# The opening loads of an encoder trunk: three parameter rows first, on ScalarE's queue, and the other rows later

## The chip, the cores and the metric

The kernel runs on one core of a Trainium2 chip. A core has five engines that run in parallel and each work through their own list of instructions in order: TensorE (PE, with its weight loads as PEld), VectorE (DVE), ScalarE (ACT), GpSimd (POOL) and SyncE (SP), which here does nothing but issue transfers. ScalarE can issue transfers too. Sixteen DMA engines move the data between HBM and the on-chip memory. An instruction waits on semaphores for what it needs, and what stands behind it on the same engine waits with it. The metric is the device time of one execution in microseconds; the median of the timed runs counts.

## What is computed

A trunk of two layers on a sequence of 1024 positions with 1024 features, in float32. Each layer norms its input, modulates it with a shift and a scale that come from a conditioning vector c, mixes over the positions (layer 0 with forgetting attention, layer 1 with gated linear attention), and then runs a gated feed-forward block in the same frame. Cut to what the change touches:

```python
c_act = jax.nn.silu(c)
for i in range(DEPTH):
    mod = c_act @ ada_w[i] + ada_b[i]
    sh1, sc1, g1, sh2, sc2, g2 = jnp.split(mod, N_MOD, axis=-1)
    h = modulate(rms_norm(x, norm1_g[i]), sh1, sc1)
    y = mixer(h)                      # layer 0: proj = h @ w_in, split into q, k, v, f_logit
    x = x + g1[:, None, :] * y
    h = modulate(rms_norm(x, norm2_g[i]), sh2, sc2)
    x = x + g2[:, None, :] * swiglu(h, ffn_w_in[i], ffn_w_out[i])
return rms_norm(x, final_g)
```

So the first product of layer 0 needs the norm of x, the vectors sh1 and sc1 (two of the six blocks of c_act @ ada_w[0], plus ada_b), norm1_g, and the weights w_in. The vectors norm2_g, gla_g_o, gla_b_a, final_g and fox_b_f are needed later.

## The kernel before

Nearly all products are split: an operand is held as a rounded high part and a low part, and a product is three matmuls (`mm3`, L260 to L263). The features are cut into 8 blocks of 128, called d, and the sequence into two halves of 512 positions, hf 0 and 1.

**Who sets the order.** The program is written as one list of instructions; a scheduler, which simulates the kernel, turns it into one list for each engine. It follows the order of the text, but lets an instruction go ahead of others that are not ready in its simulation. `tied(ins)` (L265) holds the instructions of a block behind a given instruction of the same engine. All transfers from SP go through one list; the program tracks a transfer's completion with a semaphore.

**The opening (L335 to L373).** ScalarE issues four copies of c into `craw` (L338), 32 partitions each, which become `cblk` after a Silu (L369). SP issues, in the text's order: x tile 0; the small rows of c, gla_g_o, gla_b_a and final_g into `rows2` (L342 to L345); x tile 1; the rows of ada_b, norm1_g and norm2_g into `rows` (L348 to L350); x tiles 2 and 3; the ada weights of feature 0 (`load_ada0`, L328: four transfers of 256 KB, two column blocks j times two halves kh of the inner dimension); fox_b_f into `bf` (L355), 16 pieces of 4 bytes; the weights of f, of the first q and of the first k (L216, L199), each followed in the text by its split into high and low parts; the ada weights of features 1 and 2. Then PE transposes `rows2` and `rows` into one PSUM tile `vps` (L364, L365), ScalarE makes `cact` = Silu(c) of it (L368), and DVE copies it to `vec` (L370), in which all these vectors stand as columns.

**Norm of the first half.** `ss_half(0)` (L501): ScalarE squares x tiles 0 to 3 and sums (L504), DVE and POOL make the root (L506, L507), and DVE, ScalarE and POOL scale the four tiles (L511, L513, L515).

**The loop over features (L936 to L951).** For each d, `ada0_mod(d)` (L520) makes the shift and the scale of feature d: for d = 0, 1, 2 one half of the inner dimension on PE (L527) and the other on DVE (L533, L535), for d = 3 to 7 all on DVE; then PE sums over the partitions (L537), DVE adds ada_b (L538) and makes the multiplier (`make_a`, L386). `h_block` (L541) has PE transpose the four x tiles' blocks (L544), ScalarE apply scale and shift (L546) and round (L548), and DVE or POOL make the low part (L549). `first_k` (L554) adds feature d to the products of f, q and k, `first_v` (L920) those of v, one feature later. `load_ada0(d + 3)` is issued in `pre(d)`; the ada tiles go round a ring of eleven slots, two for a feature, so that the second tile of feature 5 and all of features 6 and 7 wait until an earlier feature has been used. The two halves of the v weights (wv_0 and wv_4) come from `feed.next()` at d = 0 and d = 2. At d = 4, x tiles 4 to 7 are loaded and `ss_half(1)` follows. Behind the loop come the evacuations of the first half (`first_evac`, L881) and the same for the second half, whose features need no further modulation.

Of the kernel before, what the change touches and what calls it, by code (L numbers as in the profile page):

```python
# [16 lines left out]
P = 128  # L17
S = 1024
D = 1024
# [35 lines left out]
def trunk(ctx, tc, x, c, ada_w, ada_b, norm1_g, norm2_g, ffn_w_in, ffn_w_out,  # L55
# [139 lines left out]
    def load_w(src, name, ws=ws, lo_p=3):  # L195
# [4 lines left out]
        leave_ffn()  # L200
        w = Pair(ws([P, kk, m], FR, name + "h"), ws([P, kk, m], FR, name + "l"))
# [135 lines left out]
    for q in range(4):  # L337
        nc.scalar.dma_start(craw[32 * q:32 * q + 32], c[0].rearrange("(r s) -> r s", s=32))  # L338
    load_x(0)
    rows2 = mrows[1][0:32]  # L340
    nc.vector.memset(rows2, 0.0)
    nc.sync.dma_start(rows2[0:8, :], c.rearrange("o (j p) -> (o j) p", p=P))  # L342
    nc.sync.dma_start(rows2[8:16, :], gla_g_o.rearrange("o (j p) -> (o j) p", p=P))
    nc.sync.dma_start(rows2[16:20, :], gla_b_a.rearrange("o (j p) -> (o j) p", p=P))
    nc.sync.dma_start(rows2[20:28, :], final_g.rearrange("(j p) -> j p", p=P))  # L345
    load_x(1)
    rows = mrows[0]
    nc.sync.dma_start(rows[0:96, :], ada_b.rearrange("l (j p) -> (l j) p", p=P))  # L348
    nc.sync.dma_start(rows[96:112, :], norm1_g.rearrange("l (j p) -> (l j) p", p=P))
    nc.sync.dma_start(rows[112:128, :], norm2_g.rearrange("l (j p) -> (l j) p", p=P))  # L350
    load_x(2)
    load_x(3)
    load_ada0(0)
    bf = cst.tile([16, 1], F32, name="bf")
    nc.sync.dma_start(bf, fox_b_f.rearrange("o h -> h o"))  # L355
    W = fox_w_in[0]
    wf = load_w16(W[:, 3 * D:3 * D + 16], "fw", wst)
    wq0 = load_w(W[:, 0:P], "wq0", wst)
    wk0 = load_w(W[:, D:D + P], "wk0", wst)
# [3 lines left out]
    vps = mp0([P, 160], F32, "vps")  # L363
    nc.tensor.transpose(vps[:, P:P + 32], rows2, ident[0:32, 0:32])  # L364
# [3 lines left out]
    nc.scalar.activation(cact, vps[:, P:P + 8], AF.Silu)  # L368
    nc.scalar.activation(cblk, craw, AF.Silu)  # L369
    nc.vector.tensor_copy(vec, vps)  # L370
    gocol = lambda k: vec[:, P + 8 + k: P + 9 + k]
    fgcol = lambda k: vec[:, P + 20 + k: P + 21 + k]
    bacol = lambda k: vec[:, P + 16 + k: P + 17 + k]  # L373
# [146 lines left out]
    def ada0_mod(d):  # L520

        npe = NPE[d]
        mp = mp0([P, 2], F32, f"mp{d}")
        part = lambda k: araw[(d, k // 4)][:, k % 4]
        for j in range(2):
            for k in range(npe):
                nc.tensor.matmul(mp[:, j:j + 1], part(k)[:, j, :], cact[:, k:k + 1], start=k == 0 and j == 0,  # L527
                                 stop=k == 7 and j == 1)
# [9 lines left out]
        nc.vector.tensor_add(modc[:, 0, 0:2, d], mp, vec[:, d:d + 16:8])  # L538
# [377 lines left out]
    ss_half(0)  # L916
    acc = first_acc(0)
# [1271 lines left out]
```

## Time and profile before

| | us |
|---|---|
| three timed runs: lowest, median, highest | 2394.7, 2395.99, 2396.03 |
| the profiled execution, as timed | 2396.32 |
| its span in the trace | 2394.6 |
| PE busy in the span | 2352.3 |
| moved by the DMA engines in the first 60 us | 16.46 MB |
| mean rate of the DMA engines in the first 60 us | 274 GB/s |
| mean rate over the span | 151 GB/s |

The granted clock of TensorE was 0.997 in the mean. In the timeline a row reads: start, duration, engine, line of the kernel, operation, out<-in, count; in brackets the engine's idle time ahead of it and what ended it. `SPq` and `ACTq` are the transfers as SP and ScalarE issue them: the duration is that of the issue, not of the transfer. In the list of waits a row reads: who waited <- for whom: us in total, times, longest. In the list of transfers it reads: out<-in, issuing engine, operation, count, size of each, median us from issue to landing.

### The profile page before, as it was taken

The numbers are of one execution on the slowest core, as the hardware profiler recorded it, in microseconds if no ns is written. First come the engines' busy times: TensorE is split into PE (matmuls) and PEld (weight loads), VectorE is DVE, ScalarE is ACT, GpSimd is POOL, SyncE is SP. The second block draws the span as 40 slices with busy tenths as digits, with TensorE's granted clock in tenths as the row PEclk, the third lists the DMA queues.
The fourth block names the chain that finished last, engine by engine and source line by source line (L and its number), as shares of the span: only waits on it lengthen the run. The fifth ranks groups of instructions, "written<-read, shape, count | busy, mean of one in ns | idle before, by whom it ended". The sixth has DMA issues, their size and how long they took to land.

```text
span 2394.6 us, 35920 instructions
## 1 busy us (share of the span) xinstructions
PE 2352.3 (98%) x12246; PEld 1999.3 (83%) x12246; DVE 1679.0 (70%) x2804; ACT 1184.6 (49%) x2285; POOL 1201.8 (50%) x1073
## 2 busy tenths in 40 slices
PE   7999999999999999999999999999999999999998
PEld 6888888878888888888888898898888888888888
DVE  6577777676697778775788655345596676775787
ACT  4665556666554444445324766564443433345326
POOL 3343344432437878763363466563345666653262
PEclk9999999999999999999999999999999999999999
DMA  9233333123335555447665244454434534357664
GB/s 275 72 107 115 94 110 115 59 93 106 128 108 191 168 167 172 154 171 267 226 226 178 76 142 120 118 155 153 130 100 154 172 128 144 137 182 260 228 201 146
DMA packets 329408, 361.89 MB, mean 151 GB/s; under 512 B 24508, under 2 KB 253016, under 8 KB 329224
## 3 DMA queue, kind: packets, MB, share of 16 engines
q1 hardware_dynamic: 329032, 359.57, 46.6%
q8 instruction: 97, 1.59, 0.3%
q14 instruction: 87, 0.71, 0.1%
q10 hardware_dynamic: 192, 0.02, 0.0%
HBM read 269.25 MB, written 90.24 MB: 150 GB/s over the span
## 4 chain that ended last, share of the span: by engine, by line
PE 83%; DVE 5%; DMA 4%; ACT 3%; issue 2%; POOL 1%; SPq 1%; DVEq 0%; POOLq 0%; ACTq 0%
PE p_b L263 15%; PE p_b L262 15%; PE p_b L261 15%; PE o_b L1058 2%; PE t_b L1044 2%; PE qk_b L261 2%; PE qk_b L263 2%; PE qk_b L262 2%; PE s_b L1013 1%; PE s_b L1014 1%; PE gr_b L262 1%; PE gr_b L261 1%; PE gr_b L263 1%; PE vps_b L261 1%; PE vps_b L262 1%
## 5 line engine op out<-in xcount | busy, mean ns | idle before, releaser
L165 DVE TENSOR_TENSOR o_s<-xv_s,o_s 128x512 fp32r<-128x512 f32 (+1 forms) x376 | 343.7, 917 | 83.1 <-ACT o_s L164 82.4
L164 ACT CAST o_s<-xv_s 128x512 fp32r<-128x512 f32 (+1 forms) x376 | 217.7, 586 | 308.1 <-PE p_b L263 239.9
L1024 POOL TENSOR_SCALAR lp_s<-lp_s,st 128x128 f32<-128x128 f32 (+7 forms) x128 | 97.6, 767 | 265.9 <-DVE st L1023 229.2
L262 PE MATMUL p_b<-B,o_s 128*128 128x512 f32 x576 | 224.3, 389 | 0.0
L263 PE MATMUL p_b<-B,o_s 128*128 128x512 f32 x576 | 223.9, 389 | 0.0
L261 PE MATMUL p_b<-B,o_s 128*128 128x512 f32 x576 | 223.2, 389 | 0.0
L785 POOL TENSOR_TENSOR ex_s<-xv_s,xv_s 128x512 f32<-128x512 f32 (+1 forms) x64 | 88.3, 1380 | 259.8 <-DMA xv_s<-in_ffn_w_in_dram 89.0
L261 PE MATMUL p_b<-T,o_s 128*128 128x512 f32 x480 | 186.8, 389 | 0.0
L262 PE MATMUL p_b<-T,o_s 128*128 128x512 f32 x480 | 186.8, 389 | 0.0
L263 PE MATMUL p_b<-T,o_s 128*128 128x512 f32 x480 | 180.8, 389 | 0.0
L1022 ACT ACTIVATE lp_s<-lp_s,st 128x128 f32<-128x128 f32 (+7 forms) x128 | 99.3, 777 | 61.2 <-DVE st L1018 58.9
L261 PEld LDWEIGHTS p_b<-B,o_s 128*128 128x128 f32 x576 | 108.1, 188 | 22.5
L263 PEld LDWEIGHTS p_b<-B,o_s 128*128 128x128 f32 x576 | 108.1, 188 | 22.4
L262 PEld LDWEIGHTS p_b<-B,o_s 128*128 128x128 f32 x576 | 108.1, 188 | 22.4
L164 ACT CAST pt_s<-t_b 128x512 fp32r<-128x512 f32 (+1 forms) x160 | 79.6, 547 | 75.2 <-PE t_b L1044 74.5
L787 POOL TENSOR_TENSOR xv_s<-ex_s,xv_s 128x512 f32<-128x512 f32 (+1 forms) x64 | 84.7, 1323 | 58.1 <-DVE o_s L165 55.0
L1410 DVE TENSOR_TENSOR ex_s<-ex_s,p_b 128x512 f32<-128x512 f32 x140 | 93.6, 680 | 25.9 <-PE p_b L263 25.4
L425 POOL TENSOR_TENSOR ad_s<-ad_s,ad_s 128x512 f32<-128x512 f32 x62 | 89.1, 1438 | 34.8 <-ACT ad_s L423 22.1
L165 DVE TENSOR_TENSOR pt_s<-t_b,pt_s 128x512 fp32r<-128x512 f32 (+1 forms) x160 | 96.9, 631 | 13.8 <-ACT pt_s L164 13.5
L261 PEld LDWEIGHTS p_b<-T,o_s 128*128 128x128 f32 x480 | 90.1, 188 | 18.7
L262 PEld LDWEIGHTS p_b<-T,o_s 128*128 128x128 f32 x480 | 90.1, 188 | 18.7
L263 PEld LDWEIGHTS p_b<-T,o_s 128*128 128x128 f32 x480 | 90.1, 188 | 18.7
(1998 smaller groups left out, 7488.6 us busy)
## 6 DMA issues: line engine op xcount, KB each, us to landing
xv_s<-in_ffn_w_in_dram SPq DMA_DIRECT2D x176, 256.0 KB, 3.2
hid_B<-x SPq DMA_DIRECT2D x70, 512.0 KB, 2.7
ad_s<-in_ada_w_dram SPq DMA_DIRECT2D x384, 64.0 KB, 2.0
hid_T<-x SPq DMA_DIRECT2D x36, 512.0 KB, 2.8
xv_s<-in_ffn_w_out_dram SPq DMA_DIRECT2D x96, 192.0 KB, 4.5
ada_s<-in_ada_w_dram SPq DMA_DIRECT2D x128, 128.0 KB, 2.7
xv_s<-in_ffn_w_out_dram SPq DMA_DIRECT2D x40, 256.0 KB, 2.8
T2o<-hid_T SPq DMA_DIRECT2D x18, 512.0 KB, 8.6
```

The source lines that it names most:

```text
L164: nc.scalar.copy(hi, src)
L165: nc.vector.tensor_sub(lo, src, hi.bitcast(F32))
L261: nc.tensor.matmul(ps, ah, bh, start=start, stop=False)
L262: nc.tensor.matmul(ps, ah, bl, start=False, stop=False)
L263: nc.tensor.matmul(ps, al, bh, start=False, stop=stop)
L425: nc.gpsimd.tensor_add(acc, acc, raw)
L785: nc.gpsimd.tensor_add(s1, a21, a22)
L787: nc.gpsimd.tensor_sub(a11, s1, a11)
L1022: nc.scalar.activation(lp, lp, AF.Exp, bias=mcur, scale=-1.0, accum_out=st[:, qi, 2:3])
L1024: nc.gpsimd.tensor_scalar(lp, lp, st[:, qi, 3:4], 1.0, op0=ALU.mult, op1=ALU.mult)
L1044: nc.tensor.transpose(tp[:, i, :], lps[qi][:, psl(2 * b + jj)], ident)
L1410: nc.vector.tensor_add(d, d if src is None else dest(G, src), ps)
```

## The change

ScalarE now issues three transfers at the start, into one tile `rows` of 120 rows: c, ada_b and norm1_g. SP's list begins with x tiles 0 and 1, the four ada transfers of feature 0, x tiles 2 and 3. The weights of f, q and k are loaded as before, but their splits (`split_w16`, `split_w`) stand behind `ss_half(0)` in the text, and ScalarE's part of them is tied behind its last instruction there. Only `rows` is transposed at the start, into `vec[:, 0:112]` and `cact`. The rows of norm2_g, gla_g_o, gla_b_a and final_g, `bf`, and the four transfers of `craw` go out on SP (`later_rows`) at the end of the turn d = 1; their transpose, the copy into `vec[:, 112:148]` and the Silu of `craw` (`later_vec`) stand behind the loop over features. PE's products for the modulation of feature 1 are tied behind the instruction of PE ahead of them in the text, the last transpose of feature 0; DVE's sum for feature 0 behind its scaling of the x tiles.

```diff
+    def split_w(raw, kk, m, name, ws, lo_p=3):
         w = Pair(ws([P, kk, m], FR, name + "h"), ws([P, kk, m], FR, name + "l"))
...
-    def load_w16(src, name, ws=ws):
-
-        raw = wr([P, 8, 16], F32, name)
-        nc.sync.dma_start(raw, src.rearrange("(k p) m -> p k m", p=P))
+    def split_w16(raw, name, ws=ws):
...
-    for q in range(4):
-        nc.scalar.dma_start(craw[32 * q:32 * q + 32], c[0].rearrange("(r s) -> r s", s=32))
+    rows, rows2 = mrows[0][0:120], mrows[1][0:36]
+    bf = cst.tile([16, 1], F32, name="bf")
+    nc.scalar.dma_start(rows[112:120, :], c.rearrange("o (j p) -> (o j) p", p=P))
+    nc.scalar.dma_start(rows[0:96, :], ada_b.rearrange("l (j p) -> (l j) p", p=P))
+    nc.scalar.dma_start(rows[96:112, :], norm1_g.rearrange("l (j p) -> (l j) p", p=P))
     load_x(0)
...
     load_x(1)
...
+    load_ada0(0)
     load_x(2)
     load_x(3)
-    load_ada0(0)
...
+    def later_rows():
+        nc.sync.dma_start(rows2[0:16, :], norm2_g.rearrange("l (j p) -> (l j) p", p=P))
+        nc.sync.dma_start(rows2[16:24, :], gla_g_o.rearrange("o (j p) -> (o j) p", p=P))
+        nc.sync.dma_start(rows2[24:28, :], gla_b_a.rearrange("o (j p) -> (o j) p", p=P))
+        nc.sync.dma_start(rows2[28:36, :], final_g.rearrange("(j p) -> j p", p=P))
+        nc.sync.dma_start(bf, fox_b_f.rearrange("o h -> h o"))
+        for q in range(4):
+            nc.sync.dma_start(craw[32 * q:32 * q + 32], c[0].rearrange("(r s) -> r s", s=32))
+
+    def later_vec():
+        vps = mp0([P, 36], F32, "vps2")
+        nc.tensor.transpose(vps, rows2, ident[0:36, 0:36])
+        nc.vector.tensor_copy(vec[:, 112:148], vps)
+        nc.scalar.activation(cblk, craw, AF.Silu)
...
-    vps = mp0([P, 160], F32, "vps")
-    nc.tensor.transpose(vps[:, P:P + 32], rows2, ident[0:32, 0:32])
-    nc.tensor.transpose(vps[:, 0:P], rows, ident)
-    vec = cst.tile([P, 160], F32, name="vec")
+    vps = mp0([P, 120], F32, "vps")
+    nc.tensor.transpose(vps, rows, ident[0:120, 0:120])
+    vec = cst.tile([P, 148], F32, name="vec")
...
-    nc.scalar.activation(cact, vps[:, P:P + 8], AF.Silu)
-    nc.scalar.activation(cblk, craw, AF.Silu)
-    nc.vector.tensor_copy(vec, vps)
+    nc.scalar.activation(cact, vps[:, 112:120], AF.Silu)
+    nc.vector.tensor_copy(vec[:, 0:112], vps[:, 0:112])
...
+        behind = [last_of("P")] if d == 1 else []
...
-                nc.tensor.matmul(mp[:, j:j + 1], part(k)[:, j, :], cact[:, k:k + 1], start=k == 0 and j == 0,
-                                 stop=k == 7 and j == 1)
+                with tied(*behind):
+                    nc.tensor.matmul(mp[:, j:j + 1], part(k)[:, j, :], cact[:, k:k + 1], start=k == 0 and j == 0,
+                                     stop=k == 7 and j == 1)
...
-        nc.vector.tensor_add(modc[:, 0, 0:2, d], mp, vec[:, d:d + 16:8])
+        with tied(*[scaled] if d == 0 else []):
+            nc.vector.tensor_add(modc[:, 0, 0:2, d], mp, vec[:, d:d + 16:8])
...
     ss_half(0)
+    scaled = last_of("D")
+    with tied(last_of("A")):
+        wf = split_w16(raw_f, "fw", wst)
+        wq0, wk0 = (split_w(raw, 8, P, nm, wst) for raw, nm in zip(raw_qk, ("wq0", "wk0")))
...
+        if d == 1:
+            later_rows()
...
     for d in range(8 - VLAG, 8):
         first_v(d)
+    later_vec()
     first_evac(0, acc)
```

More of the change, by code (lines that the diff above doesn't have):

```diff
@@ L200, in load_w @@
         leave_ffn()
+        return split_w(raw, kk, m, name, ws, lo_p)
+    def split_w(raw, kk, m, name, ws, lo_p=3):
         w = Pair(ws([P, kk, m], FR, name + "h"), ws([P, kk, m], FR, name + "l"))
@@ new lines, in later_vec @@
+    def later_vec():
[3 more added lines that the diff above has]
+        nc.scalar.activation(cblk, craw, AF.Silu)
+    W = fox_w_in[0]
+    raw_f = wr([P, 8, 16], F32, "fw")
+    nc.sync.dma_start(raw_f, W[:, 3 * D:3 * D + 16].rearrange("(k p) m -> p k m", p=P))
+    raw_qk = [wr([P, 8, P], F32, nm) for nm in ("wq0", "wk0")]
+    for i, raw in enumerate(raw_qk):
+        nc.sync.dma_start(raw, W[:, i * D:i * D + P].rearrange("(k p) m -> p k m", p=P))
@@ L370, in trunk @@
[L370 to L373, printed above, removed]
+    nc.scalar.activation(cact, vps[:, 112:120], AF.Silu)
+    nc.vector.tensor_copy(vec[:, 0:112], vps[:, 0:112])
+    gocol = lambda k: vec[:, 128 + k: 129 + k]
+    bacol = lambda k: vec[:, 136 + k: 137 + k]
+    fgcol = lambda k: vec[:, 140 + k: 141 + k]
     modc = cst.tile([P, 2, 6, 8], F32, name="modc")
```

15 lines of the change are left out of this document (removed).

## The prediction

> **What bounds the kernel now.** I read the page first, for the span and the load of the engines.
>
> ```profile
> span 2394.6 us, 35920 instructions
> PE 2352.3 (98%) x12246; PEld 1999.3 (83%) x12246; DVE 1679.0 (70%) x2804; ACT 1184.6 (49%) x2285; POOL 1201.8 (50%) x1073
> ```
>
> The kernel is a TensorE kernel: its idle time is 2394.6 - 2352.3 = 42.3 us in all. The profiled execution took 2396.32 us, so 1.7 us lie around the span; the median of the three timed runs is 2395.99, 0.3 below it. All that the change touches lies in the first 70 us. There I read the table of stages (columns: stretch, its length, busy time and count for PE, PEld, DVE, ACT, POOL; then granted clock, DMA share, GB/s).
>
> ```profile
> 4.00:5.00 1.00, 0.00 (x0) 0.00 (x0) 0.00 (x0) 0.56 (x1) 0.00 (x0) 1.00 1.02 410
> 5.00:6.00 1.00, 0.00 (x0) 0.00 (x0) 0.00 (x0) 0.59 (x2) 0.00 (x0) 1.00 0.24 64
> 6.00:7.00 1.00, 0.00 (x0) 0.00 (x0) 0.00 (x0) 0.33 (x1) 0.00 (x0) 1.00 0.12 34
> 7.00:8.00 1.00, 0.28 (x1) 0.18 (x1) 0.00 (x0) 0.99 (x2) 0.00 (x0) 1.00 0.12 31
> 8.00:9.00 1.00, 0.45 (x1) 0.18 (x1) 0.00 (x0) 1.00 (x2) 0.00 (x0) 1.00 0.85 225
> 30.00:35.00 5.00, 5.00 (x30) 4.71 (x30) 4.65 (x10) 2.93 (x5) 3.80 (x5) 0.67 1.20 310
> 40.00:65.00 25.00, 21.91 (x140) 18.56 (x138) 18.45 (x40) 12.59 (x22) 14.13 (x14) 1.00 0.86 235
> 65.00:110.00 45.00, 44.99 (x259) 38.35 (x260) 23.62 (x43) 29.26 (x50) 7.86 (x8) 1.00 0.16 48
> ```
>
> The DMA engines fall almost silent from 5 to 8 us, and are as good as full at 30 us (a share over 1 is an overlap of packets in the records). From 65 us PE is busy 44.99 of 45 us and the DMA share is 0.16. So the opening is a stretch bounded by transfers, after which PE sets the time, and what the opening gains or loses goes to the end undiminished. Three waits, from the timeline of the engines, tie that stretch to the transfers:
>
> ```profile
> 42.17 1.14 ACT L207 CAST wv_4h_s<-wv_s 128x512 fp32r<-128x512 f32 x2 [6.14 <-DMA wv_s<-in_fox_w_in_dram]
> 57.43 2.73 DVE L535 SCALAR_TENSOR_TENSOR acc<-adas_s,cact,acc 128x256 f32<-128x256 f32 x3 [2.45 <-DMA adas_s<-in_ada_w_dram]
> 64.16 1.45 ACT L546 ACTIVATE y_s<-xp_b,modc,amul 128x512 f32<-128x512 f32 x2 [6.79 <-DVE amul L386]
> 64.99 1.32 PE L544 MATMUL xp_b<-ident,xt_s 128*128 128x128 f32 x8 [0.57 <-ACT y_s L546]
> ```
>
> ACT stands 6.14 us before the second half of the v weights; DVE stands 2.45 us before the last ada weights of feature 7; from there the chain goes over amul and y to PE. The stage ends when that transfer has landed.
>
> Why the DMA engines rest at 5 us shows in the timeline of SP, with ScalarE's issues ahead, and in SP's waits:
>
> ```profile
> 0.80 1.83 ACTq L338 DMA_DIRECT2D mrows_s<-in_c_dram  x4
> 0.80 0.86 SPq L323 DMA_DIRECT2D xt_s<-in_x_dram  x2
> 1.71 0.37 SPq L342 DMA_DIRECT2D mrows_s<-in_c_dram  x1
> 2.13 0.28 SPq L343 DMA_DIRECT2D mrows_s<-in_gla_g_o_dram  x1
> 3.79 0.25 SPq L344 DMA_DIRECT2D mrows_s<-in_gla_b_a_dram  x1
> 4.44 0.27 SPq L345 DMA_DIRECT2D mrows_s<-in_final_g_dram  x1
> 5.77 0.32 SPq L348 DMA_DIRECT2D mrows_s<-in_ada_b_dram  x1
> 7.06 0.90 SPq L323 DMA_DIRECT2D xt_s<-in_x_dram  x2
> 8.00 2.30 SPq L332 DMA_DIRECT2D adas_s<-in_ada_w_dram  x4
> 10.34 1.83 SPq L355 DMA_DIRECT2D bf<-in_fox_b_f_dram  x1
> ```
>
> ```profile
> SPq L344 <- DMA mrows_s<-in_c_dram: 1.4, 1, 1.4
> SPq L348 <- DMA xt_s<-in_x_dram: 1.0, 1, 1.0
> SPq L345 <- DMA xt_s<-in_x_dram: 0.4, 1, 0.4
> ```
>
> Four issues of ScalarE and four of SP go out freely. The ninth transfer, L344, waits for the landing of a first one, L345 and L348 for those of the two x tiles, though none of them needs that data. So eight transfers may be open at once, and each further one waits for the oldest. Small rows that take places between large transfers thus empty the queue: x tiles 2 and 3 go out at 7.06, with nothing left to move since 5.
>
> **The change part by part.**
>
> Start. Three rows go out on ScalarE; SP sends x 0, x 1, four ada transfers, x 2, x 3 without a small row between. Open places: three rows and five large ones; the sixth large one waits for the row of c, whose predecessor released L344 at 3.79, and by then x 0, x 1 and three ada quarters (1.8 MB) are queued, over 4 us at 410 GB/s. So the rest goes: 0.76 + 0.88 + 0.88 + 0.15 = 2.7 us of DMA time from 5 to 9 us. I take all of it, -2.7; the bounds are -2.7 and 0, the latter if another wait keeps SP. Feature 0's products, vps and cact come earlier; x 3 now stands behind 1 MB of ada weights, so the scale of the x tiles comes no earlier than now, and the gain at feature 0 is smaller than at the stream. That changes no end, since the stage ends on a transfer at 57.43.
>
> The moved rows. Nine issues (four rows, bf, four times craw) stand in program order behind feature 5's ada weights and before the second half of the v weights (L199 at 35.50 here):
>
> ```profile
> 27.61 7.79 SPq L332 DMA_DIRECT2D adas_s<-in_ada_w_dram  x8
> 35.50 1.44 SPq L199 DMA_DIRECT2D wv_s<-in_fox_w_in_dram  x1
> 36.99 5.99 SPq L332 DMA_DIRECT2D adas_s<-in_ada_w_dram  x6
> 43.03 2.25 SPq L323 DMA_DIRECT2D xt_s<-in_x_dram  x4
> 45.94 4.04 SPq L332 DMA_DIRECT2D adas_s<-in_ada_w_dram  x2
> ```
>
> ```profile
> L332 SPq DMA_DIRECT2D adas_s<-in_ada_w_dram x32: 433/832/3393, 8.0 to 49.4; - x32
> adas_s<-in_ada_w_dram SPq DMA_DIRECT2D x32, 256.0 KB, 5.7
> xt_s<-in_x_dram SPq DMA_DIRECT2D x8, 512.0 KB, 5.1
> ```
>
> A full queue takes an ada transfer each 0.83 us (the middle one of the three durations) and lands it 5.7 us after its issue (the last column of the two rows on sizes). Nine small transfers are more than the eight places: the ninth waits for the first, which lands behind all the large ones ahead of it, about 5.7 us after SP began. Meanwhile no large one follows. Then come the ninth issue, 0.3 (L344, L348), and the next large one, whose data moves 1.1 us after its issue (x 2: issued 7.06, share 0.85 in the slice from 8). The engines have run dry some 0.8 us before the landing is known (x 1: full until 5.0, known at 5.77). The gap is 0.8 + 0.3 + 1.1 = 2.2 us: the old gap again, 25 us later. It sits ahead of the v weights for which ACT waits at 42.17, of features 6 and 7, and of x 4 to 7. Queued behind it on SP are all of those, and ACT, DVE and PE in turn wait for them. Its bounds: 0, if the rows come to lie apart between large transfers, and the price of nine issues as slow as bf's, below. I take +2.2, since the start of this same trace shows just that sequence.
>
> The Trainium skill speaks against so many small transfers: "DMA: Bandwidth & Descriptors", section "Anatomy of one DMA — SWDGE (gpsimd) path", gives each a fixed 2.0 us, mostly the time until the end of the write is confirmed. It is measured on GpSimd's path; no run here shows that path. Paid one after another, nine would be 18 us by it, and the sum +15 instead of about 0; the trace speaks against this, as L342 and L343 went out 0.42 us apart. What chance that is left is part of the third rival's.
>
> The late transpose and copies. PE gets the transpose behind the loop, DVE a copy, ACT the Silu of craw; the start loses the same:
>
> ```profile
> 7.14 0.28 PE L364 MATMUL vps_b<-ident,mrows_s 32*128 32x32 f32 x1 [7.14 <-DMA mrows_s<-in_final_g_dram]
> 7.97 0.23 ACT L369 ACTIVATE cblk<-mrows_s 128x32 f32<-128x32 f32 x1
> 9.33 0.33 DVE L370 COPY vec<-vps_b 128x160 f32<-128x160 f32 x1 [6.34 <-ACT cact L368]
> ```
>
> In the start they lay beside waits for transfers; at 65 us PE's 0.28 is on the path, while ACT's 0.23 and DVE's 0.33 lie beside PE's 44.99 (without that cover +0.6). I take +0.3; bounds 0 and +0.9. The new orders (the products of feature 1 behind the transposes of feature 0, the sum of feature 0 behind the scaling, the casts of f, q and k behind the scale of x 1) hold operations to about the order that they have here: 0, bounds -0.5 and +0.5, covered by the wait at 42.17.
>
> Sum: -2.7 + 2.2 + 0.3 = -0.2 us. Against the profiled execution 2396.32 - 0.2 = 2396.1; a timed median, 0.3 below, 2395.8. What lies within 0.2%, or 4.8 us, of the time before can't be told from no change.
>
> **The rivals.**
>
> The gap does not come back. If SP's order puts the nine rows apart or into a place where SP waits anyway, the 2.7 stays: 2396.0 - 2.7 + 0.3 = 2393.6. For it speaks that SP's order is not the program's everywhere: x 1 went ahead of c's row, and x 4 to 7 at 43.03 ahead of feature 7's last two ada transfers at 45.94. Against it: all those that changed places stood behind an unready operand, and the rows wait for none. Chance 0.20.
>
> The order of the large ones tips. Feature 7's last pair might now go ahead of x 4 to 7. Those are four times 512 KB, 2.1 MB, 5.1 us at 410 GB/s; the wait at 57.43 would go. Of that PE can use only its idle time in this stretch, 25.00 - 21.91 = 3.1 us in the row from 40 to 65, beside the 2.7 of an earlier start: at most 2396.1 - 5.8 = 2390.3, and 2391.5 if four fifths of it are had.  Speaks for it: the pair is held by a place in the ring that PE and DVE free, both earlier now. Against: x 4 to 7 then land later, and the second half waits for them. Chance 0.12.
>
> Slow issues in a full queue (the slower side). bf's issue, 16 pieces of 4 bytes, took 1.83 us at 10.34 behind a full queue. Place: the nine issues ahead of the v weights. At 0.83 each they take 7.5 us, the gap is 7.5 + 1.1 - 4.9 = 3.7 and the result 2397.3; at 1.83 each 16.5 us, a gap of 12.7 and 2406.3. It decides over the rest of the queue (5.7 us) from 0.63 us an issue, and makes the kernel slower by 4.8 from (4.8 + 2.4 + 3.8) / 9 = 1.2. Against: behind the fast two at 1.71 and 2.13 the queue was full as well. Chance 0.13; in 0.07 it is over 4.8.
>
> A colder PE. With a longer wait at 42 us PE could fall to the low clock again: the row from 30 us has a granted clock of 0.67, which costs 5 x 0.33 = 1.65 us. The Trainium skill, "TensorE: Matmul & The Clock Gate", section "Part 1: The HAM clock gate (the "warmup" mystery)", has the clock fall after about 3.4 us of idling; this trace has the low clock in a row in which PE is busy 5.00 of 5.00, so recorded activity alone doesn't decide. It would shift the forecast to 2397.5; I give it 0.1 of the forecast's own 0.55.
>
> **How the numbers follow.** The forecast, a moved gap, has 0.55: 2395.8. With the rivals' 0.20, 0.12 and 0.13 that is all. The range of 8 in 10 reaches from 2391.0, in the tipped order, to 2399.5, with the colder PE and the issues at 0.83 together (2395.8 + 1.65 + 1.5 = 2399.0, and the scatter of the runs). Faster by over 0.2% only by the tipped order, 0.09 of its 0.12; slower by over 0.2%, 0.07; between them 0.84.
>
> **What would show it.** Right: the DMA share stays at 0.9 or over from 3 to 30 us; nine small issues follow one another on SP before the second v weights, with a stretch of 2 to 3 us of low DMA share behind them; ACT's wait for wv_4 is longer than 6.14 us and its end near 42; DVE's wait for feature 7 ends at 57 to 58. Wrong: DVE's wait ends at 55 or earlier (the gap did not return), the last ada pair is issued ahead of x 4 to 7 (tipped), or issues of over 1.2 us among the nine (slow queue). A difference that arises behind 110 us would mean that the order of the later work changed, which I price at nothing; that would break the forecast most thoroughly.

## The result, and the profile after

| | us |
|---|---|
| the changed kernel, median of 13 runs (lowest to highest) | 2402.63 (2400.98 to 2403.46) |
| the kernel before in the same runs, median of 13 | 2396.78 |
| ratio, with its 95% interval | 1.0025 (1.0017 to 1.0033) |
| profiled execution of the changed kernel, as timed | 2402.99 |

The change makes the kernel 5.85 us slower (0.25%). The interval of the ratio does not reach 1, and the time lies above the range that was given. The head of the page after:

```profile
span 2401.2 us, 35924 instructions
PE 2357.7 (98%) x12246; PEld 2002.2 (83%) x12246; DVE 1678.6 (70%) x2804; ACT 1185.6 (49%) x2285; POOL 1203.9 (50%) x1073
```

PE has the same matmuls and is busy 5.4 us longer (2352.3 before): some of them ran slower. The stages of the changed kernel, columns as in the prediction's table (length, busy time of PE, PEld, DVE, ACT, POOL, then granted clock, DMA share, GB/s):

```profile
3.00:5.00 2.00, 0.00 (x0) 0.00 (x0) 0.00 (x0) 0.82 (x2) 0.00 (x0) 1.00 0.93 356
5.00:8.00 3.00, 0.43 (x1) 0.18 (x1) 0.00 (x0) 2.53 (x5) 0.00 (x0) 1.00 1.14 319
8.00:30.00 22.00, 17.80 (x86) 16.31 (x87) 15.21 (x30) 9.44 (x16) 9.87 (x11) 1.00 1.19 299
...
35.00:36.00 1.00, 0.79 (x6) 0.76 (x6) 0.29 (x1) 1.00 (x3) 0.77 (x2) 1.00 0.26 61
36.00:37.00 1.00, 1.00 (x8) 0.97 (x8) 1.00 (x2) 0.97 (x2) 1.00 (x2) 0.88 0.07 14
37.00:38.00 1.00, 1.00 (x6) 0.87 (x5) 0.96 (x2) 0.01 (x1) 0.73 (x1) 0.50 0.06 8
38.00:39.00 1.00, 0.38 (x1) 0.00 (x0) 0.96 (x3) 0.06 (x1) 0.00 (x0) 0.50 0.25 23
39.00:40.00 1.00, 0.82 (x2) 0.72 (x3) 0.96 (x3) 0.17 (x1) 0.00 (x0) 0.50 0.82 196
40.00:65.00 25.00, 20.41 (x114) 17.58 (x113) 18.87 (x42) 12.28 (x21) 14.00 (x14) 0.84 0.86 244
65.00:110.00 45.00, 44.42 (x246) 38.40 (x247) 18.16 (x30) 28.33 (x47) 8.03 (x8) 0.93 0.07 20
110.00:2401.00 2291.00, 2267.50 (x11777) 1924.54 (x11775) 1618.33 (x2678) 1128.78 (x2192) 1166.99 (x1029) 1.00 0.46 150
```

Read the DMA share first. The silence from 5 to 8 us has gone (1.14), and it is back from 35 to 39 (0.26, 0.07, 0.06, 0.25), as the prediction had it for the transfers. Then read PE and its clock. From 40 to 65 us PE is busy 20.41 us at a mean clock of 0.84, where before had 21.91 at 1.00. Behind 110 us PE idles 2291 - 2267.5 = 23.5 us; before, it idled 2284 - 2260.3 = 23.7 us there:

```profile
110.00:2394.00 2284.00, 2260.27 (x11731) 1919.73 (x11729) 1613.98 (x2665) 1126.47 (x2190) 1165.51 (x1029) 1.00 0.46 150
```

So nothing is lost there; the loss arises between 30 and 75 us.

The timeline of SP shows the nine rows, and SP's waits what held them:

```profile
12.15 15.20 SPq L334 DMA_DIRECT2D adas_s<-in_ada_w_dram  x17
27.47 0.76 SPq L199 DMA_DIRECT2D wv_s<-in_fox_w_in_dram  x1
...
30.90 0.87 SPq L351 DMA_DIRECT2D mrows_s<-in_norm_g_dram  x1
...
32.23 0.25 SPq L353 DMA_DIRECT2D mrows_s<-in_gla_b_a_dram  x1
...
34.53 0.32 SPq L355 DMA_DIRECT2D bf<-in_fox_b_f_dram  x1
35.42 2.26 SPq L357 DMA_DIRECT2D mrows_s<-in_c_dram  x4
37.79 0.39 SPq L199 DMA_DIRECT2D wv_s<-in_fox_w_in_dram  x1
```

```profile
SPq L355 <- DMA wv_s<-in_fox_w_in_dram: 1.7, 1, 1.7
SPq L357 <- DMA adas_s<-in_ada_w_dram: 1.4, 3, 0.6
```

One thing there was not forecast. The first v weights (L199 at 27.47) stand behind 17 ada transfers; before had 12 ahead of them. PE waits for their cast:

```profile
35.21 0.50 PE L942 MATMUL vps_b<-wv_0h_s,h0h 128*128 128x256 f32 x2 [2.07 <-ACT wv_0h_s L211]
```

Rows that answer to the prediction's waits, from the timelines of ACT and of DVE:

```profile
41.76 1.14 ACT L211 CAST wv_4h_s<-wv_s 128x512 fp32r<-128x512 f32 x2 [2.59 <-DMA wv_s<-in_fox_w_in_dram]
```

```profile
56.91 3.34 DVE L546 SCALAR_TENSOR_TENSOR acc<-adas_s,cact,acc 128x256 f32<-128x256 f32 x3 [1.24 <-DMA adas_s<-in_ada_w_dram]
```

Both waits end 0.4 to 0.5 us earlier than before (42.17 and 57.43). The prediction let the stage end on "a transfer at 57.43"; that transfer is in time, and the stage ends later all the same. The reason stands in two other timelines. GpSimd, before and then after:

```profile
55.77 1.28 POOL L549 TENSOR_TENSOR h0l<-y_s,h0h 128x512 fp32r<-128x512 f32 x1
...
58.60 5.43 POOL L515 TENSOR_SCALAR xt_s<-xt_s,rstd 128x1024 f32<-128x1024 f32 x4
```

```profile
57.41 5.07 POOL L524 TENSOR_SCALAR xt_s<-xt_s,rstd 128x1024 f32<-128x1024 f32 x4
...
64.37 1.25 POOL L561 TENSOR_TENSOR h0l<-y_s,h0h 128x512 fp32r<-128x512 f32 x1
```

Feature 5's low part (h0l) stood ahead of the scaling of x tiles 4 to 7; now it stands behind it and starts 8.6 us later. PE after, in the same stretch:

```profile
62.59 0.52 PE L556 MATMUL xp_b<-ident,xt_s 128*128 128x128 f32 x3 [0.36 <-POOL xt_s L524]
...
68.04 0.63 PE L569 MATMUL fs_b<-h0l,fw_s 128*128 128x512 f32 x1
```

PE's list too has the second half's transposes, which wait for the scaled tiles, ahead of feature 5's low products (L569). While they wait PE has next to nothing, and then its clock falls; the stages of after in slices of 1 us:

```profile
60.00:61.00 1.00, 0.00 (x0) 0.00 (x0) 1.00 (x3) 0.00 (x0) 1.00 (x1) 1.00 0.02 4
61.00:62.00 1.00, 0.35 (x4) 0.38 (x4) 0.57 (x2) 0.33 (x1) 1.00 (x2) 1.00 0.00 0
62.00:63.00 1.00, 0.64 (x6) 0.45 (x5) 0.00 (x0) 0.97 (x2) 1.00 (x2) 1.00 0.00 0
63.00:64.00 1.00, 0.16 (x2) 0.05 (x1) 0.84 (x3) 0.10 (x1) 1.00 (x2) 1.00 0.06 16
64.00:65.00 1.00, 0.62 (x2) 0.27 (x2) 0.53 (x2) 0.46 (x1) 1.00 (x2) 0.53 0.00 0
65.00:66.00 1.00, 0.63 (x3) 0.63 (x4) 0.00 (x0) 0.97 (x3) 0.94 (x2) 0.50 0.55 158
66.00:67.00 1.00, 0.79 (x5) 0.39 (x4) 0.00 (x0) 0.97 (x2) 0.92 (x3) 0.50 0.88 256
...
69.00:70.00 1.00, 1.00 (x4) 0.81 (x3) 0.30 (x1) 0.67 (x2) 0.78 (x1) 0.50 0.00 0
70.00:71.00 1.00, 1.00 (x4) 0.77 (x4) 1.00 (x1) 0.00 (x0) 0.50 (x1) 0.55 0.00 0
71.00:72.00 1.00, 1.00 (x6) 0.83 (x5) 0.05 (x1) 0.00 (x0) 0.00 (x0) 1.00 0.00 0
```

From 64 to 71 us the clock is 0.50 to 0.55, also where PE is busy all the time.

### The profile page after: what moved, and what is told of

It reads as the page before. It is cut to its first block, busy times and chain, and to the rows that moved or that the text cites. A ratio compares the mean times of both kernels' runs of the same rounds, so it can differ in the third digit from the quotient of the medians.

```text
span 2401.2 us, 35924 instructions
## 1 busy us (share of the span) xinstructions
PE 2357.7 (98%) x12246; PEld 2002.2 (83%) x12246; DVE 1678.6 (70%) x2804; ACT 1185.6 (49%) x2285; POOL 1203.9 (50%) x1073
## 4 chain that ended last, share of the span: by engine, by line
PE 83%; DVE 5%; DMA 4%; ACT 3%; issue 2%; POOL 2%; SPq 0%; DVEq 0%; POOLq 0%; ACTq 0%
PE p_b L265 15%; PE p_b L264 15%; PE p_b L263 15%; PE o_b L1077 2%; PE t_b L1063 2%; PE qk_b L263 2%; PE qk_b L264 2%; PE qk_b L265 2%; PE s_b L1032 1%; PE s_b L1033 1%; PE gr_b L265 1%; PE vps_b L263 1%; PE vps_b L265 1%; PE vps_b L264 1%; PE gr_b L264 1%
```

## The experiments

The profile of after shows three changed places in the lists that could be the cause: the late first v weights on SP, the sums of features 3 and 6 on DVE behind something that waits, feature 5's low part on POOL. The rivals: the moved gap, or the new loads themselves. Each time stands beside the median of the kernel before in the same runs. The last column is a second measure, read from the profiled executions: how much later than in before (198.72 us) ACT starts one cast of v weights (`wv_0h_s`) that stands behind all of the changed work. It leaves out what a single execution gains or loses after that.

| kernel | us | before | ratio (95%) | cast later by, us |
|---|---|---|---|---|
| b_loads_only | 2395.66 | 2396.45 | 0.9995 (0.9987 to 1.0004) | +0.92 |
| c_wv0_first | 2402.90 | 2396.45 | 1.0028 (1.0019 to 1.0037) | +8.15 |
| d_feature7_behind | 2410.67 | 2396.45 | 1.0055 (1.0041 to 1.0069) | +15.34 |
| e_rows_end | 2398.09 | 2396.45 | 1.0008 (0.9999 to 1.0016) | +3.75 |
| f_splits_only | 2395.75 | 2396.39 | 0.9997 (0.9988 to 1.0006) | +0.06 |
| g_low5_late | 2403.96 | 2396.39 | 1.0033 (1.0021 to 1.0046) | +8.30 |
| h_low5_first | 2402.80 | 2396.39 | 1.0025 (1.0016 to 1.0034) | +7.68 |
| i_low5_rows_end | 2402.06 | 2396.39 | 1.0018 (1.0009 to 1.0027) | +6.52 |
| j_tie_only | 2402.76 | 2396.08 | 1.0029 (1.0018 to 1.0041) | +6.28 |
| k_without_tie | 2399.12 | 2396.08 | 1.0010 (1.0000 to 1.0019) | +4.04 |
| l_wv0_low5 | 2403.08 | 2396.08 | 1.0029 (1.0017 to 1.0040) | +8.27 |
| m_loads_rows_end | 2394.14 | 2396.08 | 0.9991 (0.9982 to 1.0000) | -0.73 |
| n_sum3_late | 2395.24 | 2396.67 | 0.9993 (0.9985 to 1.0002) | +1.26 |
| o_low5_late_b | 2401.79 | 2396.67 | 1.0022 (1.0013 to 1.0031) | +6.77 |
| p_both_late | 2402.02 | 2396.67 | 1.0021 (1.0012 to 1.0030) | +6.84 |
| q_wv4_pool | 2402.95 | 2396.67 | 1.0025 (1.0016 to 1.0034) | +7.48 |
| r_low5_vector | 2401.08 | 2396.29 | 1.0019 (1.0010 to 1.0027) | +4.93 |
| s_low5_vector_rows_end | 2398.75 | 2396.29 | 1.0009 (1.0000 to 1.0018) | +3.44 |

In after that cast is 7.75 us late (206.47).

### Which part of the change loses: b, f, j, k

b_loads_only: all the new loads, the late rows and the late transpose; the splits stand where before had them, and no tie.

```diff
-    raw_f = wr([P, 8, 16], F32, "fw")
...
+    wf = load_w16(W[:, 3 * D:3 * D + 16], "fw", wst)
+    wq0 = load_w(W[:, 0:P], "wq0", wst)
+    wk0 = load_w(W[:, D:D + P], "wk0", wst)
...
-        behind = [last_of("P")] if d == 1 else []
...
-        with tied(*[scaled] if d == 0 else []):
-            nc.vector.tensor_add(modc[:, 0, 0:2, d], mp, vec[:, d:d + 16:8])
+        nc.vector.tensor_add(modc[:, 0, 0:2, d], mp, vec[:, d:d + 16:8])
...
-    with tied(last_of("A")):
-        wf = split_w16(raw_f, "fw", wst)
```

> The changed kernel with its new order of loads and its late rows, but with the splits of f, q and k back in front of the x norm and without the three ties; the first v weights then go out on SP ahead of feature 4's ada weights, as in the kernel before. Order theory (the loss comes from the place of the first v weights in SP's list and of feature 6's sum in DVE's list): the first loss of PE, some 8 us between 32 and 48 us, is gone, that at feature 6 and 7 is still there; 2396 to 2400 us. Gap theory (the loss comes from the stretch of empty DMA queues behind the nine rows): the gap is unchanged, so 2402 us as in the changed kernel.

Measured 2395.66: nothing lost that can be told from the scatter. The empty stretch is there as in after. PE works through it at full clock and pays right behind it: it runs out for 2.4 us, and then its clock falls. Three stages of b:

```profile
35.00:40.00 5.00, 5.00 (x33) 4.47 (x32) 3.14 (x9) 0.23 (x1) 0.00 (x0) 1.00 0.20 35
40.00:45.00 5.00, 2.58 (x21) 2.29 (x20) 1.97 (x3) 2.43 (x4) 2.48 (x4) 1.00 1.15 319
45.00:50.00 5.00, 5.00 (x26) 4.53 (x25) 4.79 (x12) 1.38 (x2) 1.41 (x1) 0.66 1.09 373
```

POOL keeps feature 5's low part (56.34) ahead of the scaling (from 57.64) in b, as before had it.

f_splits_only: the other half, the loads of before with the moved splits and the three ties.

```diff
 (the loads of before)
+    raw_f = wr([P, 8, 16], F32, "fw")
...
+    with tied(last_of("A")):
+        wf = split_w16(raw_f, "fw", wst)
+        wq0, wk0 = (split_w(raw, 8, P, nm, wst) for raw, nm in zip(raw_qk, ("wq0", "wk0")))
```

> The loads of before, with only the moved splits of f, q and k and the three ties of the change. In this build the list of GpSimd keeps feature 5's low part ahead of the scaling of x tiles 4 to 7, and SyncE's list is that of before. Theory (the loss comes from where feature 5's low part lands on GpSimd, and from what the open stretch of the queue then uncovers): no loss, 2395.5 to 2397.5 us against 2396.4. Rival (the moved splits and the ties cost by themselves): 2399 to 2402.5 us, most of the 5.85 us that the whole change lost.

Measured 2395.75: nothing lost either. Each half alone is harmless; only together do they lose. But the lists of all five engines are here those of before, in their first 400 rows: with the old loads the three ties change no order. So f does not show what such an order would cost with the old loads.

j_tie_only and k_without_tie take the ties apart.

```diff
 (j_tie_only)
-        behind = [last_of("P")] if d == 1 else []
+        behind = []
...
-        with tied(*[scaled] if d == 0 else []):
+        with tied(*[]):
```

> The changed kernel with two of its three ties taken out again (feature 1's products behind the transposes, feature 0's sum behind the scaling); only the tie of the casts of f, q and k behind the last scaling of ScalarE stays. In the build all lists but four rows of VectorE's are those of the changed kernel. Theory (that one tie holds the whole loss): 2401 to 2404 us, as the changed kernel. Rival (the loss is shared by the three ties): at least 2 us less, 2397 to 2400.5 us.

```diff
 (k_without_tie)
-    with tied(last_of("A")):
+    with tied():
         wf = split_w16(raw_f, "fw", wst)
```

> The changed kernel without the tie of the casts of f, q and k behind ScalarE's last scaling; the other two ties stay. SyncE's list is then that of b_loads_only (first v weights behind 12 transfers of ada_w, not 17); on GpSimd one x tile is scaled ahead of feature 5's low part, which should end some 1.3 us later than in b_loads_only. Theory: the loss goes, 2395 to 2397.5 us. Rival (the loss comes with the new loads as soon as any splits are moved): 2400 to 2403 us.

j measured 2402.76: the tie of the casts of f, q and k behind ScalarE's last scaling carries the whole loss by itself. k measured 2399.12, above what was expected: 3.6 us of j's loss go with that tie, but 3 stay (the interval of their ratio reaches from nothing to 4.6). In the lists as built, taking the tie of feature 1's products away as well leaves those of b_loads_only but for four rows of DVE, so by the lists these 3 us belong to that second tie; beside the first one it changes no list at all. And with none of the three ties the first 400 rows of every engine's list are b's, row by row: that the splits moved in the text did nothing.

### Through which places the tie acts: c, d, h, l, q, r and g, n, o, p

Taking one place out of the changed kernel. c_wv0_first puts the first v weights back behind 12 transfers; further ties, left out here, keep the nine rows behind feature 5's ada weights and x tiles 4 to 7 behind feature 7's first pair:

```diff
-            load_ada0(d + 3)
+            with tied(*wv_at):
+                load_ada0(d + 3)
...
             wvs[0] = [feed.next()]
+            wv_at.append(last_of("S"))
```

> The changed kernel with the ada weights of features 4 to 7 tied on SP behind the first v weights, and the nine rows behind feature 5's ada weights, where they are in the changed kernel. Order theory: PE no longer stands at 33 us, the granted clock returns to 1.0 from 35 us on, 3 to 5 us less than the changed kernel, 2397.5 to 2399.5 us. Gap theory: the rows and the gap stay, 2402 us.

Measured 2402.90. The wait for the first v weights at 34 us has gone, and PE stands later instead:

```profile
44.58 1.01 PE L548 MATMUL mp_b<-ones,acc 128*128 128x1 f32 x4 [3.44 <-DVE modc L550]
```

d_feature7_behind ties feature 7's products on DVE behind feature 6's sum:

```diff
-        for k in range(npe, 8):
+        with tied(*last_a if d == 7 else []):
+            for k in range(npe, 8):
...
         make_a(0, 0, slice(d, d + 1))
+        last_a[:] = [last_of("D")]
```

> The changed kernel with DVE's products of feature 7 tied behind the sum and multiplier of feature 6. Order theory: feature 6 is done some 3 us earlier, PE does not stand at 60 us; 2 to 4 us less than the changed kernel, 2398.5 to 2400.5 us, while the wait at 33 us stays. Gap theory: 2402 us.

Measured 2410.67, 8 us slower than after. That place was not the cause, and the tie made things worse: DVE now stands 2.93 us for PE ahead of the sum, at 57.36, with feature 7's products queued behind it.

h_low5_first ties the scaling on POOL behind feature 5's low part; l_wv0_low5 does so in c; i_low5_rows_end in e (below).

```diff
-                nc.gpsimd.tensor_scalar(xt[t], xt[t], r, 1.0, op0=ALU.mult, op1=ALU.mult)
+                with tied(*low5):
+                    nc.gpsimd.tensor_scalar(xt[t], xt[t], r, 1.0, op0=ALU.mult, op1=ALU.mult)
...
+            low5.append(last_of("G"))
             ss_half(1)
```

> The changed kernel with the scaling of x tiles 4 to 7 tied behind feature 5's low part on GpSimd; transfers as in the changed kernel. GpSimd's four low parts of the first q and k weights (3 us) still stand ahead of it, so it should end near 60 instead of 65.6 us. Theory: 3 to 4.5 us back, 2398 to 2399.6 us, the rest of the loss staying with the open stretch of the queue. Rival (GpSimd's order is harmless): 2401.5 to 2403.5 us.

> c_wv0_first (2402.9 us) with the scaling of x tiles 4 to 7 tied behind feature 5's low part as well. Theory that the orders on SyncE and GpSimd are the two ends of the loss: 3 to 5 us less than c_wv0_first, 2398 to 2400 us. Rival, from h_low5_first and i_low5_rows_end: mending single orders by ties only moves the wait into TensorE's later list (70 to 85 us): 2401.5 to 2404 us.

Measured 2402.80 and 2403.08. The stretch from 55 to 70 us is mended and nothing is won. Two stages of after, the same two of h, and PE's waits in h's second one:

```profile
55.00:70.00 15.00, 11.00 (x57) 8.96 (x56) 8.13 (x14) 8.23 (x14) 13.65 (x14) 0.80 0.44 103
70.00:90.00 20.00, 20.00 (x110) 16.97 (x110) 7.26 (x12) 11.66 (x20) 3.08 (x3) 0.98 0.00 1
```

```profile
55.00:70.00 15.00, 14.28 (x95) 12.78 (x94) 6.68 (x12) 5.43 (x10) 13.00 (x13) 1.00 0.44 106
70.00:90.00 20.00, 17.90 (x95) 14.35 (x94) 8.01 (x14) 15.71 (x28) 3.87 (x3) 1.00 0.00 1
```

```profile
77.62 0.47 PE L263 MATMUL ks_b<-h0h,wk0h_s 128*128 128x512 f32 x1 [0.73 <-DVE KLB L737]
81.35 0.39 PE L263 MATMUL vps_b<-wv_0h_s,h0h 128*128 128x256 f32 x1 [1.24 <-DVE v_s L165]
```

PE is busy 14.28 of 15 us where after had 11.00, but then 17.90 of 20 where after had 20.00: it has done more by 70 us, and then waits for the accumulators of the first half, which DVE clears. At 200 us nothing of it is left: the cast starts at 206.40, in after at 206.47.

q_wv4_pool takes the wait for the second v weights off DVE, so that feature 3's sum runs at 40.59 instead of 43.39; r_low5_vector computes feature 5's low part on DVE.

```diff
 (q_wv4_pool)
-            wvs[0].append(feed.next())
+            f, *a = feed.loads.popleft()
+            wvs[0].append(f(*a, ws, 4))
```

> The changed kernel with all four low parts of the second v weights on GpSimd, so that nothing on VectorE waits for them ahead of feature 3's sum; SyncE's list as in the changed kernel, GpSimd still has feature 5's low part behind the scaling. Theory of overlap: little comes back, 2401.5 to 2403.5 us, since the later wait takes in the earlier. Rival (the terms add up): 2 to 3 us back, 2399.3 to 2400.8 us.

```diff
 (r_low5_vector)
-        (nc.gpsimd if d % 2 == 1 else nc.vector).tensor_sub(lo, y, hi.bitcast(F32))
+        (nc.gpsimd if d % 2 == 1 and (d, hf) != (5, 0) else nc.vector).tensor_sub(lo, y, hi.bitcast(F32))
```

> The changed kernel with feature 5's low part computed on VectorE instead of GpSimd, so that it can't stand behind the scaling of x tiles 4 to 7; no tie added. TensorE's list then has 8 of the second half's transposes ahead of feature 7's products, where before has 16. Theory (that place is necessary for the loss as well as sufficient): 3 to 6 us back, 2396.5 to 2399.5 us. Rival, from h_low5_first: the wait at 58 us goes, but the evacuation of the first half then holds TensorE at 75 to 85 us, and the time stays at 2401.5 to 2403.5 us.

Measured 2402.95 and 2401.08. Neither gives the loss back; r has 1 us of it by the medians (4.8 above before in its runs, after 5.85) and 2.8 by the cast. None of the places tried is necessary for the loss.

Putting one place into a kernel that lost nothing. g_low5_late is the kernel before, with only feature 5's low part issued behind the scaling:

```diff
+        if d == 5 and hf == 0:
+            late5.append(lambda: nc.gpsimd.tensor_sub(lo, y, hi.bitcast(F32)))
+            return
         (nc.gpsimd if d % 2 == 1 else nc.vector).tensor_sub(lo, y, hi.bitcast(F32))
...
             ss_half(1)
+            with tied(last_of("G")):
+                late5[0]()
```

> The kernel before with one thing changed: feature 5's low part is issued on GpSimd behind the scaling of x tiles 4 to 7 (and the matmuls that read it stand later in TensorE's list). All transfers as before. Theory: 3 to 5 us slower, 2399.5 to 2401.5 us, with TensorE short of work between 58 and 68 us. Rival (the whole loss is the open stretch of the queue and the late first v weights, and GpSimd's order is harmless): 2396 to 2397 us.

Measured 2403.96, +7.6: more than expected. SP's list is that of before, row by row. The stage from 55 to 70 us, in before and then in g:

```profile
55.00:70.00 15.00, 13.46 (x80) 11.21 (x81) 6.81 (x9) 8.15 (x14) 13.99 (x14) 1.00 0.41 97
```

```profile
55.00:70.00 15.00, 7.24 (x27) 5.73 (x28) 6.92 (x11) 6.61 (x11) 13.09 (x14) 0.66 0.40 101
```

Nearly half of PE's busy time is gone from it, and a third of the clock. Where PE stands in g, from its timeline:

```profile
58.77 0.33 PE L546 MATMUL xp_b<-ident,xt_s 128*128 128x128 f32 x1 [1.86 <-POOL xt_s L515]
63.41 0.98 PE L537 MATMUL mp_b<-ones,acc 128*128 128x1 f32 x4 [4.32 <-DVE acc L535]
...
67.02 0.78 PE L562 MATMUL fs_b<-h0l,fw_s 128*128 128x512 f32 x1
```

The low part itself is 1.43 us, issued 7.2 us later (62.96). What counts is what went with it: the products of feature 5 (L562) left the place in PE's list where they had covered PE's two waits, for the scaled tiles and for the last sums, which hang on the last ada weights. This edit can't part POOL's place from PE's, as PE's list follows it.

n_sum3_late, o_low5_late_b and p_both_late do the same to b_loads_only: n with feature 3's sum behind the second v weights' low part on DVE, o with feature 5's low part as in g, p with both.

```diff
 (n_sum3_late; o has the edit of g, p both)
             wvs[0].append(feed.next())
+            wv4.append(last_of("D"))
...
-        nc.vector.tensor_add(modc[:, 0, 0:2, d], mp, vec[:, d:d + 16:8])
+        with tied(*(wv4 if d == 3 else [])):
+            nc.vector.tensor_add(modc[:, 0, 0:2, d], mp, vec[:, d:d + 16:8])
```

> b_loads_only (2395.66 us) with feature 3's sum tied behind the second v weights' low part on VectorE, where the changed kernel has it; the lists of SyncE, ScalarE and GpSimd stay. Theory (a term of its own: TensorE gets feature 3's block some 2.4 us later, in a stretch in which nothing else is ready): 2 to 3 us slower, 2397.5 to 2399 us. Rival (TensorE waits for the second v weights there anyway): 2395 to 2396.5 us.

> b_loads_only with feature 5's low part issued on GpSimd behind the scaling of x tiles 4 to 7, as in g_low5_late but with the new loads. Theory (this place is a term of about 7.6 us whatever the loads): 2401.5 to 2404 us. Rival (it costs that only with the transfers of before): 2396 to 2399 us.

> b_loads_only with both: feature 3's sum behind the second v weights' low part, and feature 5's low part behind the scaling. No tie of the casts of f, q and k. Theory (the two places make up the loss of the changed kernel, and they overlap, the later one taking in the earlier): 2401.5 to 2404 us, as the changed kernel. Rival (they add up): 2404.5 to 2407 us. Third possibility (the loss needs the late first v weights too): below 2400.5 us.

n measured 2395.24: feature 3's sum costs nothing, though PE now waits 3.79 us for it. In b it waited 2.42 us there for a cast. PE's timeline in n, then in b:

```profile
43.53 0.58 PE L544 MATMUL mp_b<-ones,acc 128*128 128x1 f32 x4 [3.79 <-DVE modc L546]
```

```profile
44.34 0.50 PE L561 MATMUL fs_b<-h0h,fw_s 128*128 128x512 f32 x1 [2.42 <-ACT h0h L553]
```

o measured 2401.79 and p 2402.02: feature 5's low part, with the products that follow it, turns the harmless kernel into one as slow as after, within 1 us (ratios 1.0022 and 1.0025). The traces show the place: up to its products PE in o is 1.2 us behind b, as one more cold stretch left it; the first of them (L562 in b) starts at 57.72 in b and at 63.50 in o, 5.8 us later.

### What the open stretch is worth: e, i, m, s

e_rows_end is the changed kernel with the nine rows behind feature 7's last pair (and x tiles 4 to 7 tied behind its first); i is e with h's tie, s is e with r's edit, and m_loads_rows_end is b_loads_only with the rows there.

```diff
 (e_rows_end; in m without the tie of the x tiles)
-        if d == 1:
-            later_rows()
+        if d == 3:
+            ada7 = [last_of("S", 2), last_of("S")]
...
-            for t in range(4, 8):
-                load_x(t)
+            with tied(ada7[0]):
+                for t in range(4, 8):
+                    load_x(t)
...
+    with tied(ada7[1]):
+        later_rows()
     later_vec()
```

> The changed kernel with the nine rows issued behind the last ada transfer of feature 7, and x tiles 4 to 7 tied behind that feature's first two, so that all other transfers keep their order. No gap is left ahead of the second v weights, and every transfer behind it lands 2 to 3 us earlier. Order theory: PE still stands for the first v weights at 33 us, at the low clock, and feature 6 still waits behind feature 7 on DVE, but less long; 2399.5 to 2401.5 us. Gap theory: the loss was the gap's, 2396 us or less.

> The changed kernel with both: the nine small rows behind the last pair of feature 7 (as in e_rows_end, 2398.1 us) and the scaling tied behind feature 5's low part. Theory: the two add up, 2398.1 - 3.5 = 2394.6 us, 2393.5 to 2395.6, faster than before. Rival (GpSimd's order is harmless): as e_rows_end, 2397 to 2399 us.

> b_loads_only (2395.66 us) with the nine small rows behind the last pair of feature 7 and no tie but that one; GpSimd keeps feature 5's low part ahead of the scaling. Theory (the open stretch of the queue behind the nine small issues is worth what the prediction gave it, 2.2 to 2.7 us, and there is no other loss): 2393 to 2394 us, the fastest of all. Rival (the stretch is hidden in this order of work, TensorE being fed from what has come already): 2395 to 2396.5 us.

> e_rows_end (2398.1 us) with feature 5's low part on VectorE: neither the open stretch of the queue nor the place behind the scaling is left. Theory: 2393 to 2396 us, as m_loads_rows_end (2394.1). Rival, from i_low5_rows_end (2402.1): TensorE's list as the tie of the casts leaves it holds the evacuation back, 2400 to 2403 us.

e measured 2398.09, 4.5 us less than after: above what one of its two theories expected and below what the other did. Of the transfers, only the rows change their place from after to e, and feature 5's low part still stands behind the scaling there (61.87, the scaling from 55.37). i measured 2402.06 and s 2398.75: again the mended low part brings nothing, even where the stretch is full; i is 4 us slower than e. m measured 2394.14, the fastest of all, 1.9 us under before; its interval ends at 1.0000. From b to m the two ratios differ by 0.0004, within their intervals, so the stretch's price without the ties is about 1 us, and may be anything from nothing to some 4. (In m two of the x tiles also go out earlier than in b.) The stage of m:

```profile
30.00:40.00 10.00, 10.00 (x48) 9.00 (x48) 7.54 (x18) 2.57 (x5) 2.77 (x4) 1.00 1.16 318
```

The DMA share is 1.16 (after 0.72 in the same ten microseconds), and PE is busy throughout at full clock.

Four kernels form a square, with and without the three ties, with the rows in the middle or at the end. By the medians, against before: m -1.9, b -0.8, e +1.7, after +5.85. By the cast: m -0.7, b +0.9, e +3.8, after +7.8. So the rows in the middle cost 1 to 2 us without the ties and about 4 with them; the ties cost about 4 us with the rows at the end and about 7 with the rows in the middle. The two do not simply add: after loses most where both meet.

## Why the prediction was wrong

The step that failed is this one: "The new orders (...) hold operations to about the order that they have here: 0, bounds -0.5 and +0.5, covered by the wait at 42.17". One of these orders, the casts of f, q and k behind the scale of x 1, brings the whole loss by itself with the new loads: +6.7 us in j. It holds the three casts themselves by about one scaling. But the lists of all engines are fixed ahead of the run, by a planner that orders by what it takes to be ready. A late cast frees its raw buffer later; there are three, so the first v weights go behind 17 transfers instead of 12; and from there on all five lists differ. A second of these orders, feature 1's products behind the transposes, costs some 3 us where the first is missing (k, and by the lists). Shown: that the tie of the casts does it (j), that with the old loads the ties change no order (f), and that one of the places it changes is enough by itself (o, and g with the transfers of before). Shown too: that the loss is not the tie's alone, as moving the nine rows with all ties in place takes 4.5 of the 5.85 us back (e). The prediction added the rows and the orders as separate terms, and they are not. Argued from the lists only: the way from the cast to that place. Open: which set of places the changed kernel needs for its loss. The low part behind the scaling is sufficient and not necessary: with it mended (h, l, r) other waits come up, at 44 us or at 77 to 82.

The cover was wrong as well. "The wait at 42.17" can hide only what is late before 42; feature 5's low part is late at 64. A changed order goes on behind the wait that was to cover it.

The steps on transfers held as far as the order of events goes. b_loads_only is the prediction's sum -0.2 without the ties: 2395.66 beside 2396.45, where -0.8 can't be told from -0.2. That the sum fits there confirms neither term, as the next figures show. By rows: a DMA share of 0.93 or over from 3 to 30 us; nine small issues ahead of the second v weights; then low share from 35 to 39. The gap was sized too small: the shares leave 0.74 + 0.93 + 0.94 + 0.75 + 0.18 = 3.5 us, not 2.2, of which the kernel loses 1 to 2 without the ties and about 4 with them. Nor does what the opening gains always go "to the end undiminished": in m, ACT's cast of v weights at 109.40 in before starts at 105.32, 4.1 us earlier, and the one at 198.72 at 197.99, only 0.7 earlier. Not the ninth issue alone waited: bf waited 1.7 us and the parts of craw 1.4 in three waits, for v and ada transfers that were still open. The last ada weights of feature 7 ended DVE's wait at 56.91, just short of "57 to 58". The wait for wv_4 was 2.59 instead of over 6.14, because ACT itself came late to it, and ended at 41.76 as forecast.

Of the rivals, "the gap does not come back" is m, built by hand: 2393.6 forecast, 2394.14 measured. The tipped order did not occur in after: x tiles 4 to 7 (42.88) still went out ahead of feature 7's last pair (45.60). Slow issues did not occur in after: the nine took 0.25 to 0.87 us each. "A colder PE" was right as a thing that happens and too small: 1.65 us were allowed for one cold stretch; the stretch from 64 to 71 us alone has about 6.8 us at half clock, some 3 us of PE's work, an estimate from the 1 us slices. It is hardly a cause of its own: added up from such slices, after has 20.5 us at half clock and j 10.3, at lists that differ in a few rows of DVE, and the two profiled executions are only 1.3 us apart (2402.99 and 2401.66). Most of these stretches follow one in which PE had run out; the one from 30 to 33 us in after does not (PE is busy in each slice from 27 on), and why the clock fell there stays open.

The Trainium skill, "TensorE: Matmul & The Clock Gate", section "Part 1: The HAM clock gate (the "warmup" mystery)", says that the clock has two states, half and full, and changes after about 3.4 us of idling or of sustained work. The 1 us slices of after agree on the states: 0.50 and 1.00, and 0.53 and 0.55 where a slice holds a change. They agree on the length: added up from the slices, the four stretches at half clock in after last 3.4, 6.8, 3.4 and 6.8 us, once or twice the figure. In the last one PE is busy 0.6 to 0.8 in the first three slices and all the time from 67, some 3.9 us before the clock is back. On the fall they agree only in part: ahead of the one at 64 us PE is busy 0.00, 0.35, 0.64 and 0.16, so it was not idle throughout, and ahead of the one at 30 us it is busy all the time.

The prediction also asked what would break it most: a difference behind 110 us. After has none (23.5 us of idle PE there, before 23.7); the break was in the stage that it had read, on engines that it had not followed.

## What to carry to other kernels

A tie between two instructions is an edit of every list behind them: before pricing it by the operations that it names, ask which buffer they free, what is loaded into that buffer, and which engine's in-order list holds something small that PE needs soon behind something large that it needs later. Look for that last pattern directly: here one low part of 1.3 us behind four scalings, 5 us together, and with it the matmuls that had covered PE's waits, cost 6 to 8 us (o and g), more than any transfer moved. And mend the cause, not the places: seven kernels that set single places right by further ties or moves (c, d, h, i, l, q, r) stayed 4.8 to 14 us above before, while leaving the ties out and laying the small rows behind the last large transfer gave the fastest kernel by the median (m, whose interval just reaches no change). And do not price two moves of one stage apart: with the ties in place, the nine rows cost about 4 us where they cost 1 to 2 without.

## What the runs showed of the hardware

The half clock can outlast the wait ahead of it: about 4 us of a starving PE (60 to 64 us in after) were followed by 6.8 us at 0.50 to 0.55, in which PE was busy 0.6 to 0.8 in the first three slices and all the time in the rest. The stretches at half clock came in steps of 3.4 us (added up from the slices): 3.4 and 6.8 us in after, 3.4 in before, 3.4 and 10.2 in g; m had none between 8 and 110 us. An average busy share does not show them (98% before and after); the granted clock by slices does.

A small transfer's issue was mostly cheap (0.25 to 0.87 us for the nine rows in after; but 2.71 us for the first of them in m, and 1.83 us for bf in before), and its place in the queue dear: nine of them, ahead of a large one, left 3.5 us of the DMA engines' time empty.
